# A hybrid decoder layer on one core: the opening loop's instruction order pinned on TensorE, ScalarE and VectorE, and the last shift sum moved to TensorE

## The chip, the cores and the metric

The kernel runs on 1 core of one Trainium2 chip. The metric is device time of one execution in microseconds; lower is better. The kernel before takes 2865.55 us, the median of 3 runs (2865.07 to 2865.57). The profile shown here is of one further execution, which took 2869.29 us.

## The reference, cut to what matters

One decoder layer over 512 tokens of 2048 channels, in float32. The opening stage, which the change touches, computes the normalised and conditioned input `h` and its first products:

```python
mod = jax.nn.silu(c) @ w_ada + b_ada
shift, scale, gate = jnp.split(mod[:, None, :], 3, axis=-1)
h = rms_norm(x, norm_w) * (1.0 + scale) + shift
proj = h @ w_in
```

Behind it stand a sliding-window attention branch, a gated delta-rule branch and their gated merge, all of which read `h`. `c` is one vector of 2048, so `silu(c) @ w_ada` is a product of one row with a 2048 x 6144 matrix: every weight is loaded for one multiplication.

## The kernel before, in words

`h` is kept transposed: channels on the 128 partitions, in `KT` = 16 channel tiles of 128, and the 512 tokens along the free side. A product in float32 is made of three matmuls. Each operand is split into a rounded high part and the remainder (`whi` and `wlo` of the weights, `hh` and `hl` of `h`), and the kernel adds `hh*whi`, `hl*whi` and `hh*wlo` in PSUM. ScalarE makes the high part by a copy, and VectorE the low part by a subtraction that reads it.

The function `startup` is the opening stage. It loads `x` in four blocks, normalises and transposes it into `xnT` (up to about 28 us), and then walks the 16 channel tiles. For tile `kt` these steps are needed:

- **The sums** (line 450, and 441 to 447). Two numbers for each of the tile's 128 channels: index `j` = 0 is the shift, 1 the scale. Each is a dot product of 2048 weights with `silu(c)`. On VectorE one is a multiplication over a 128 x 2048 tile `wa` with an accumulated output, written here as sum(kt, j). The shift of even tiles is instead made on TensorE: 16 small matmuls into the PSUM tile `ada` (line 441), a copy to `adas` by ScalarE (446), and a last matmul with the vector `pick` that adds four partial rows (447). For those tiles the weights are stored in another layout.
- **adaln(kt)** (lines 455 to 469). Two VectorE instructions on 128 x 1, here sh0 (line 459, the shift) and sh1 (line 463, the scale), then on ScalarE `h` (468) and its rounded copy `hh` (469).
- **low(kt)** (line 473): `hl` on VectorE.
- **The weight split**: `whi` (line 53, ScalarE) and `wlo` (line 54, VectorE) of the tile's 128 x 832 weights of `w_st`, one half of a load `raw`.
- **products(kt)**: seven outputs accumulate in PSUM over all 16 tiles: two value tiles `v`, one tile `ba`, four key tiles `k`. With three matmuls each that is 21 matmuls per tile (lines 275 to 277).

In the loop, pass `kt` writes adaln(kt+1), the sums of kt+2, low(kt+1) and the products of kt. That is only the order in which the source names them. A scheduler of the framework then sets the order on each engine by its own estimate of when things are ready, and the engines run their lists in that order, each waiting at its next instruction until its inputs are there.

The weights of the sums come in 32 loads of 1 MB into six buffers `wa`; the loads for tile kt+3 go into the buffers of tile kt, so their issue waits until sum or matmuls of tile kt have read them. The loads `raw` (832 KB, one for two tiles) have two buffers; the issue waits for the second `wlo` of the load two before. All are issued by SyncE's queue in order. After the loop come `ba`, the two `vt` copies and the next stage (`mm` tiles, lines 275 to 277 again), in which TensorE works through the large weight matrices.

Of the kernel before, what the change touches and what calls it, by code (L numbers as in the profile page):

```python
# [36 lines left out]

class Layer:
# [339 lines left out]
    def startup(self, st):  # L378


        tc, nc, a, const = self.tc, self.nc, self.a, self.const
# [4 lines left out]

        def load_ada(kt):
            for j in range(2):
                wa = s2.tile([P, D], F32, tag="wa", name="wa", bufs=6)
# [22 lines left out]
        scr = sp.tile([P, KT, 32], F32, name="silu_cr")  # L412
        nc.vector.tensor_copy(out=scr, in_=self.sc.unsqueeze(2).to_broadcast([P, KT, 32]))
        scb = sp.tile([P, D], F32, name="silu_cb")
        for q in range(4):
# [4 lines left out]
            nc.scalar.copy(out=scb[:, q * T : (q + 1) * T], in_=ps.rearrange("p c n -> p (c n)"))  # L420
        pick = sp.tile([P, 1], F32, name="pick")
        nc.vector.memset(pick, 0.0)
        for g in range(4):
# [7 lines left out]
        ada = pa.tile([P, T], F32, name="ada")

        def ada_sums(kt):


            t = acc[kt] = s2.tile([P, 2], F32, tag="acc", name="acc")
            if kt % 2 == 0:
                w = loads[kt, 0].rearrange("p (k n) -> p k n", k=KT)
                for k in range(4):
                    for g in range(4):  # L440
                        nc.tensor.matmul(
                            ada[32 * g : 32 * g + 32, 0:P], lhsT=scr[:, 4 * k + g, :], rhs=w[:, 4 * k + g, :],
                            start=k == 0, stop=k == 3,
                        )
                sb = s2.tile([P, P], F32, tag="adas", name="adas", bufs=1)
                nc.scalar.copy(out=sb, in_=ada[:, 0:P])
                nc.tensor.matmul(ada[:, P : P + 1], lhsT=sb, rhs=pick, start=True, stop=True)
            for j in (1, 0)[: 1 + kt % 2]:
                wa = loads[kt, j]
                nc.vector.scalar_tensor_tensor(  # L450
                    out=wa, in0=wa, scalar=1.0, in1=scb, op0=ALU.mult, op1=ALU.mult, accum_out=t[:, j : j + 1]
                )
                yield

        def adaln(kt):

            t = acc[kt]
            sh = s2.tile([P, 2], F32, tag="sh", name="sh")
            nc.vector.tensor_scalar(
                out=sh[:, 0:1], in0=t[:, 0:1] if kt % 2 else ada[:, P : P + 1], scalar1=self.b_ada[:, kt : kt + 1],  # L460
                scalar2=None, op0=ALU.add,
            )
            nc.vector.tensor_scalar(
                out=sh[:, 1:2], in0=t[:, 1:2], scalar1=self.norm_w[:, kt : kt + 1], scalar2=bn[:, kt : kt + 1],
                op0=ALU.mult, op1=ALU.add,
            )
            h32 = s2.tile([P, T], F32, tag="h32", name="h32")
            nc.scalar.activation(h32, xnT[:, kt, :], AF.Identity, scale=sh[:, 1:2], bias=sh[:, 0:1])
            nc.scalar.copy(out=self.hh[:, kt, :], in_=h32)
            return h32  # L470

        def low(kt, h32):
            nc.vector.tensor_tensor(
                out=self.hl[:, kt, :], in0=h32, in1=self.hh[:, kt, :].bitcast(F32), op=ALU.subtract
            )

        n = 0
        for tb in range(NTB):
# [8 lines left out]
            for q in range(4):  # L487
                i = n % 7
                ps = pa.tile([P, 4, P], F32, tag=f"x{i}", name="xtp") if i < 3 else self.psc.tile([P, 4, P], F32, tag="sc", name="xtp")
# [6 lines left out]
                    nc.scalar.copy(out=dst, in_=ps)  # L496
                n += 1

        def products(kt, parts):
            f, l = kt == 0, kt == KT - 1  # L500
            wh, wl = parts
            x = (self.hh[:, kt, :], self.hl[:, kt, :])
            for ps, o, n in outs:
                self.mm3(ps, (wh[:, o : o + n], wl[:, o : o + n]), x, f, l)

        list(ada_sums(0))
        low(0, adaln(0))
        list(ada_sums(1))
# [1280 lines left out]
```

## Time and profile before

| What | Value |
|---|---|
| Median of 3 runs | 2865.55 us |
| The profiled execution | 2869.29 us, span 2867.5 us |
| TensorE busy, share of the span | 2819.6 us, 98% |
| VectorE, ScalarE, GpSimd busy | 64%, 41%, 9% |
| Data moved | 590.09 MB, mean 206 GB/s |
| First matmul of the loop's products | 31.29 us |
| First matmul of the next stage (`mm`) | 144.55 us |
| VectorE multiplications of 128 x 2048 (line 450) | 24, mean 2283 ns |

Times in the trace count from the start of the span. A row of the timeline has the start, the duration, the engine, the line, the operation and the tiles (written before read, buffer numbers left out). A bracket behind it says how long the engine was idle before that row and what ended the wait. Durations overlap in the engines' pipelines, so the cost of an instruction in a row of them is the distance from its start to the next start, not its own duration.

### The profile page before, as it was taken

How to read it: one execution, taken by the hardware profiler on the slowest of the kernel's cores; microseconds unless marked ns; L12 is line 12 of the kernel's file. 1: busy time of each engine (PE TensorE's matmuls, PEld its weight loads, DVE VectorE, ACT ScalarE, POOL GpSimd, SP SyncE). 2: the span in 40 equal slices, each digit the busy share in tenths (PEclk: the TensorE clock that was granted, in tenths of full speed). 3: DMA queues.
4: the chain of work that ended last, by engine and by line, in shares of the span. 5: the costliest groups of instructions: out<-in, count | busy, mean ns of one | idle time of the engine just before them, and what ended most of it. 6: DMA issues, size and time to landing. Idle time of an engine off the chain costs nothing.

```text
span 2867.5 us, 38132 instructions
## 1 busy us (share of the span) xinstructions
PE 2819.6 (98%) x14364; PEld 2321.4 (81%) x14364; DVE 1824.3 (64%) x2882; ACT 1176.7 (41%) x2289; POOL 271.1 (9%) x266
## 2 busy tenths in 40 slices
PE   7899999999999999999999999999999999999999
PEld 6687788788888888888888888888887778788887
DVE  6765988877775555566665456666556655554575
ACT  4354333344444444444443455443343434442343
POOL 0022111101102111111100000000100100000000
PEclk9999999999999999999999999999999999999999
DMA  9757555636768777878873477675645647365575
GB/s 377 291 190 204 171 174 156 199 103 198 222 195 249 204 229 232 252 232 245 248 209 102 145 257 264 242 258 187 224 149 164 176 140 218 121 226 176 203 233 163
DMA packets 205807, 590.09 MB, mean 206 GB/s; under 512 B 74900, under 2 KB 99988, under 8 KB 154424
## 3 DMA queue, kind: packets, MB, share of 16 engines
q1 hardware_dynamic: 195416, 529.46, 54.1%
q0 software_dynamic: 10208, 58.20, 10.5%
q8 instruction: 113, 1.85, 0.3%
q14 instruction: 70, 0.57, 0.1%
HBM read 523.79 MB, written 166.40 MB: 241 GB/s over the span
## 4 chain that ended last, share of the span: by engine, by line
PE 88%; DVE 6%; DMA 2%; ACT 2%; issue 1%; SPq 0%; POOL 0%; DVEq 0%; POOLq 0%; ACTq 0%
PE mm L275 21%; PE mm L277 20%; PE mm L276 20%; PE od L276 3%; PE od L275 3%; PE od L277 3%; PE m L277 2%; PE m L276 2%; PE m L275 2%; DVE wa L450 1%; PE S L1425 1%; DVE wlo L54 1%; DVE A L886 1%; PE po L1057 1%; DVE atmp L879 1%; PE O L1476 1%
## 5 line engine op out<-in xcount | busy, mean ns | idle before, releaser
L275 PE MATMUL mm<-hh,whi 128*128 128x512 f32 x2784 | 1125.0, 404 | 5.5 <-ACT mth L298 4.6
L277 PE MATMUL mm<-hh,wlo 128*128 128x512 f32 x2784 | 1089.7, 391 | 2.7 <-DVE wlo L54 2.7
L276 PE MATMUL mm<-hl,whi 128*128 128x512 f32 x2784 | 1088.0, 391 | 0.0
L54 DVE TENSOR_TENSOR wlo<-raw,whi 128x1024 fp32r<-128x1024 f32 (+1 forms) x476 | 586.9, 1236 | 504.5 <-ACT whi L53 503.1
L53 ACT CAST whi<-raw 128x1024 fp32r<-128x1024 f32 (+1 forms) x476 | 496.8, 1047 | 797.1 <-PE mm L276 651.5
L275 PEld LDWEIGHTS mm<-hh,whi 128*128 128x128 f32 x2784 | 524.4, 188 | 118.9 <-issue 9.6
L277 PEld LDWEIGHTS mm<-hh,wlo 128*128 128x128 f32 x2784 | 523.4, 188 | 116.3 <-DVE wlo L54 3.9
L276 PEld LDWEIGHTS mm<-hl,whi 128*128 128x128 f32 x2784 | 524.9, 189 | 102.6 <-issue 1.4
L276 PE MATMUL od<-wlo,oh 128*128 128x512 f32 x448 | 174.6, 390 | 0.4 <-DVE wlo L54 0.4
L275 PE MATMUL od<-whi,oh 128*128 128x512 f32 x448 | 174.8, 391 | 0.0
L277 PE MATMUL od<-whi,ol 128*128 128x512 f32 x448 | 174.4, 389 | 0.0
L834 POOL TENSOR_TENSOR E<-E,neg_g 128x512 f32<-128x512 f32 x64 | 74.5, 1163 | 928.3 <-DMA E<-g_rows 804.6
L886 DVE TENSOR_TENSOR A<-A,atmp 128x62 f32<-128x62 f32 (+30 forms) x124 | 113.6, 916 | 1.7
L879 DVE TENSOR_TENSOR atmp<-A 128x62 f32<-128x62 f32 (+30 forms) x124 | 112.9, 911 | 1.6
L276 PEld LDWEIGHTS od<-wlo,oh 128*128 128x128 f32 x448 | 84.1, 188 | 17.9 <-DVE wlo L54 0.8
L277 PEld LDWEIGHTS od<-whi,ol 128*128 128x128 f32 x448 | 84.1, 188 | 17.6
L275 PEld LDWEIGHTS od<-whi,oh 128*128 128x128 f32 x448 | 84.1, 188 | 17.1
L54 DVE TENSOR_TENSOR wlo<-raww,whi 128x1024 fp32r<-128x1024 f32 x56 | 68.4, 1223 | 45.5 <-ACT whi L53 45.4
L53 ACT CAST whi<-raww 128x1024 fp32r<-128x1024 f32 x56 | 59.2, 1057 | 81.8 <-PE m L277 71.9
L988 POOL TENSOR_TENSOR qe<-qe,yq 128x512 f32<-128x512 f32 x32 | 49.8, 1577 | 420.1 <-DMA qe<-eg_rows 249.5
L1059 ACT COPY osb<-po 128x256 f32<-128x256 f32 x64 | 23.9, 373 | 126.9 <-PE po L1057 126.8
L1043 ACT ACTIVATE vs<-pv,kd 128x128 f32<-128x128 f32 x96 | 30.1, 366 | 107.0 <-PE pv L1039 107.0
(341 smaller groups left out, 3273.2 us busy)
## 6 DMA issues: line engine op xcount, KB each, us to landing
raw<-in_w_ch SPq DMA_DIRECT2D x158, 1024.0 KB
wa<-in_w_ada_ss SPq DMA_DIRECT2D x32, 1024.0 KB
od_m<-in_w_od POOLq DMA_DIRECT2D x32, 1024.0 KB, 10.9
raw<-od_m SPq DMA_DIRECT2D x32, 1024.0 KB
raw<-in_w_od SPq DMA_DIRECT2D x24, 1024.0 KB
E<-g_rows SPq DMA_DIRECT2D x64, 256.0 KB
od_m<-in_w_od SPq DMA_DIRECT2D x16, 1024.0 KB
od_m<-od_m SPq DMA_DIRECT2D x16, 1024.0 KB
```

Source lines behind the costliest of these rows:

```text
L53: self.nc.scalar.copy(out=hi, in_=src)
L54: self.nc.vector.tensor_tensor(out=lo, in0=src, in1=hi.bitcast(F32), op=ALU.subtract)
L275: nc.tensor.matmul(ps, lhsT=wh, rhs=xh, start=first, stop=False)
L276: nc.tensor.matmul(ps, lhsT=wh, rhs=xl, start=False, stop=False)
L277: self.last_mm = nc.tensor.matmul(ps, lhsT=wl, rhs=xh, start=False, stop=last).ins
L450: nc.vector.scalar_tensor_tensor(out=wa, in0=wa, scalar=1.0, in1=scb, op0=ALU.mult, op1=ALU.mult, accum_out=t[:, j : j + 1])
L834: self.in_turn(nc.gpsimd.tensor_tensor(out=E, in0=E, in1=ng, op=ALU.add))
L879: eng.tensor_tensor(out=t, in0=A[:, m : m + 1, m + 1 :].to_broadcast([P, m, n]), in1=A[:, :m, m : m + 1].to_broadcast([P, m, n]), op=ALU.mult,
L886: eng.tensor_tensor(out=A[:, :m, m + 1 :], in0=A[:, :m, m + 1 :], in1=t, op=ALU.add)
L988: self.in_turn(nc.gpsimd.tensor_tensor(out=qf, in0=qf, in1=q, op=ALU.mult))
L1043: nc.scalar.activation(vs[:, e, :], pv[:, e, :], AF.Copy, scale=self.kd[:, c, 2 * g + e : 2 * g + e + 1])
L1057: m = nc.tensor.matmul(po[:, e, :], lhsT=M[e][:, c, :], rhs=vn[:, e, :], start=c == 0, stop=True)
```

## The change

A helper `turn` adds an ordering edge from each instruction to the last one given to it for the same engine; the edge asks for an order only, not for a wait. With it the loop's order is written out for three engines:

- **VectorE**, in pass kt: sh1(kt+1), sh0(kt+1), wlo(kt+1), hl(kt+1), then the sums of kt+2.
- **ScalarE**: whi(kt+1), the copy `adas` where tile kt+1 has its shift on TensorE, h(kt+1), hh(kt+1).
- **TensorE**: the 16 small matmuls of tile kt+1, then the products of kt, output by output with the order `hh*whi`, `hl*whi`, `hh*wlo`; the matmul with `pick` stands after the first two outputs.

Only one half of weights is split ahead, where the scheduler was free to take several. Of the last tile, 15, the shift sum moves from VectorE to TensorE (`SHIFT_PE`), so VectorE has 23 multiplications of 128 x 2048 in place of 24. After the loop one split of weights is made as before. The core of the diff:

```diff
+SHIFT_PE = (0, 2, 4, 6, 8, 10, 12, 14, 15)
...
+        def turn(op, queue="dve"):
+
+            if queue in last:
+                self.tc.add_manual_dep(
+                    op.ins, last[queue],
+                    mybir.DependencyInfo(mybir.DependencyClass.NoSync, mybir.DependencyReason.DATA), reason="turn",
+                )
+            last[queue] = op.ins.name
+
+        def shift_sum(kt):
+
+
+            if kt not in SHIFT_PE:
+                return
...
+                    turn(nc.tensor.matmul(
+                        ada[32 * g : 32 * g + 32, 0:P], lhsT=scr[:, 4 * k + g, :], rhs=w[:, 4 * k + g, :],
+                        start=k == 0, stop=k == 3,
+                    ), "pe")
+            sb = s2.tile([P, P], F32, tag="adas", name="adas", bufs=1)
+            turn(nc.scalar.copy(out=sb, in_=ada[:, 0:P]), "act")
+            return sb
...
-            for j in (1, 0)[: 1 + kt % 2]:
+            for j in (1,) if kt in SHIFT_PE else (0, 1):
                 wa = loads[kt, j]
-                nc.vector.scalar_tensor_tensor(
+                turn(nc.vector.scalar_tensor_tensor(
                     out=wa, in0=wa, scalar=1.0, in1=scb, op0=ALU.mult, op1=ALU.mult, accum_out=t[:, j : j + 1]
-                )
-                yield
+                ))
...
+            weights(kt, parts)
+            turn(nc.vector.tensor_tensor(
                 out=self.hl[:, kt, :], in0=h32, in1=self.hh[:, kt, :].bitcast(F32), op=ALU.subtract
-            )
+            ))
...
+            for i, (ps, o, n) in enumerate(outs):
+                if i == 2:
+                    to_channels(sb)
+                for a, b in ((wh, x[0]), (wh, x[1]), (wl, x[0])):
+                    m = nc.tensor.matmul(
+                        ps, lhsT=a[:, o : o + n], rhs=b, start=f and b is x[0] and a is wh, stop=l and a is wl
+                    )
+                    turn(m, "pe")
...
         for kt in range(KT):
-            nxt = kt + 1 < KT and adaln(kt + 1)
+            parts = kt + 1 < KT and cast(kt + 1)
             if kt + 3 < KT:
                 load_ada(kt + 3)
-            sums = ada_sums(kt + 2) if kt + 2 < KT else iter(())
-            next(sums, None)
-            if kt + 1 < KT:
-                low(kt + 1, nxt)
-            list(sums)
-            products(kt, self.half(f"st{kt // 2}"))
-            self.half_done()
+            products(kt, shift_sum(kt + 1))
+            if parts:
+                adaln(kt + 1, parts)
+            if kt + 2 < KT:
+                sums(kt + 2)
             self.weight_tick()
+        self.split_half()
```

VectorE's list from hl(7) to hl(9), in the kernel before. `hl` with `h32` is a tile's low part, `wa` with `acc` a sum, `sh` from `ada` or from `acc` with `b_adaT` is sh0, `sh` with `norm_wT` is sh1:

```order
L473 TENSOR_TENSOR hl_68<-h32_679,hh_67 128x512
L459 TENSOR_SCALAR sh_733<-ada_175,b_adaT_105 128x1
L450 SCALAR_TENSOR_TENSOR wa_643,acc_686<-wa_643,silu_cb_140 128x2048
L463 TENSOR_SCALAR sh_733<-acc_686,norm_wT_107,bn_171 128x1
L54 TENSOR_TENSOR wlo_771<-raw_670,whi_770 128x832
L54 TENSOR_TENSOR wlo_828<-raw_670,whi_827 128x832
L473 TENSOR_TENSOR hl_68<-h32_736,hh_67 128x512
L450 SCALAR_TENSOR_TENSOR wa_682,acc_743<-wa_682,silu_cb_140 128x2048
L459 TENSOR_SCALAR sh_774<-acc_743,b_adaT_105 128x1
L450 SCALAR_TENSOR_TENSOR wa_684,acc_743<-wa_684,silu_cb_140 128x2048
L463 TENSOR_SCALAR sh_774<-acc_743,norm_wT_107,bn_171 128x1
L473 TENSOR_TENSOR hl_68<-h32_777,hh_67 128x512
```

The same stretch, hl(7) to hl(9), in the changed kernel:

```order
L507 TENSOR_TENSOR hl_68<-h32_707,hh_67 128x512
L470 SCALAR_TENSOR_TENSOR wa_623,acc_712<-wa_623,silu_cb_140 128x2048
L495 TENSOR_SCALAR sh_763<-acc_712,norm_wT_107,bn_171 128x1
L499 TENSOR_SCALAR sh_763<-ada_175,b_adaT_105 128x1
L484 TENSOR_TENSOR wlo_717<-raw_616,whi_716 128x832
L507 TENSOR_TENSOR hl_68<-h32_766,hh_67 128x512
L470 SCALAR_TENSOR_TENSOR wa_679,acc_771<-wa_679,silu_cb_140 128x2048
L470 SCALAR_TENSOR_TENSOR wa_681,acc_771<-wa_681,silu_cb_140 128x2048
L495 TENSOR_SCALAR sh_802<-acc_771,norm_wT_107,bn_171 128x1
L499 TENSOR_SCALAR sh_802<-acc_771,b_adaT_105 128x1
L484 TENSOR_TENSOR wlo_775<-raw_616,whi_774 128x832
L507 TENSOR_TENSOR hl_68<-h32_805,hh_67 128x512
```

The work is the same: three sums, two `wlo`, two `hl`. Before, both `wlo` stand in the step to the even tile and none in the step to the odd one. Now each step has one, between sh0 and `hl`.

TensorE's list at the start of products(7) in the kernel before, from the small matmuls of tile 8 on:

```order
L441 MATMUL ada_175<-wa_641,silu_cr_138 32x128 x16
L275 MATMUL v0_371<-hh_67,whi_729 128x512
L275 MATMUL v1_372<-hh_67,whi_729 128x512
L447 MATMUL ada_175<-pick_165,adas_703 128x1
L276 MATMUL v0_371<-hl_68,whi_729 128x512
L277 MATMUL v0_371<-hh_67,wlo_730 128x512
```

The same place in the changed kernel:

```order
L453 MATMUL ada_175<-wa_719,silu_cr_138 32x128 x16
L541 MATMUL v0_375<-hh_67,whi_774 128x512
L541 MATMUL v0_375<-hl_68,whi_774 128x512
L541 MATMUL v0_375<-hh_67,wlo_775 128x512
L541 MATMUL v1_376<-hh_67,whi_774 128x512
L541 MATMUL v1_376<-hl_68,whi_774 128x512
L541 MATMUL v1_376<-hh_67,wlo_775 128x512
L463 MATMUL ada_175<-pick_165,adas_837 128x1
```

The second matmul of the products now reads `hl`, where it was the third or a later one, and the matmul with `pick` stands behind six matmuls in place of two. SyncE's list of loads keeps its order except that the third `raw` load now stands ahead of the two loads for tile 4. Behind the loop the lists differ in a few places of the gate computation and in the place of one `raw` load only.

More of the change, by code (lines that the diff above doesn't have):

```diff
@@ L431, in startup @@
         ada = pa.tile([P, T], F32, name="ada")
-        def ada_sums(kt):
-            t = acc[kt] = s2.tile([P, 2], F32, tag="acc", name="acc")
[L437 to L443, printed above, removed]
-                        )
-                sb = s2.tile([P, P], F32, tag="adas", name="adas", bufs=1)
-                nc.scalar.copy(out=sb, in_=ada[:, 0:P])
-                nc.tensor.matmul(ada[:, P : P + 1], lhsT=sb, rhs=pick, start=True, stop=True)
-            for j in (1, 0)[: 1 + kt % 2]:
+        last = {}
@@ new lines, in turn @@
+        def turn(op, queue="dve"):
[8 more added lines that the diff above has]
+                return
+            w = loads[kt, 0].rearrange("p (k n) -> p k n", k=KT)
+            for k in range(4):
+                for g in range(4):
+                    turn(nc.tensor.matmul(
[5 more added lines that the diff above has]
+            return sb
@@ L449, in ada_sums, with to_channels, sums @@
+        def to_channels(sb):
+            if sb is not None:
+                turn(nc.tensor.matmul(ada[:, P : P + 1], lhsT=sb, rhs=pick, start=True, stop=True), "pe")
+        def sums(kt):
+            t = acc[kt] = s2.tile([P, 2], F32, tag="acc", name="acc")
+            for j in (1,) if kt in SHIFT_PE else (0, 1):
                 wa = loads[kt, j]
-                nc.vector.scalar_tensor_tensor(
+                turn(nc.vector.scalar_tensor_tensor(
                     out=wa, in0=wa, scalar=1.0, in1=scb, op0=ALU.mult, op1=ALU.mult, accum_out=t[:, j : j + 1]
-                )
@@ L453, in ada_sums, with cast, weights @@
-                yield
-        def adaln(kt):
+                ))
+        def cast(n):
+            w = self.jobs[n // 2][1].shape[-1] // 2
+            hi = self.whl.tile([P, 1024], F32R, tag="whi", name="whi")
+            lo = self.whl.tile([P, 1024], F32R, tag="wlo", name="wlo")
+            src = self.raws[n // 2][:, (n % 2) * w : (n % 2 + 1) * w]
+            turn(nc.scalar.copy(out=hi[:, :w], in_=src), "act")
+            return hi, lo, src, w
+        def weights(n, parts):
+            hi, lo, src, w = parts
+            turn(nc.vector.tensor_tensor(out=lo[:, :w], in0=src, in1=hi[:, :w].bitcast(F32), op=ALU.subtract))
+            self.halves[n] = (hi, lo)
+            self.half_split += 1
+            if n % 2:
+                del self.raws[n // 2], self.raw_in[n // 2]
+                self.due.append(self.load_job)
@@ L457, in adaln @@
+        def adaln(kt, parts):
             t = acc[kt]
             sh = s2.tile([P, 2], F32, tag="sh", name="sh")
[L459 to L463, printed above, removed]
+            turn(nc.vector.tensor_scalar(
                 out=sh[:, 1:2], in0=t[:, 1:2], scalar1=self.norm_w[:, kt : kt + 1], scalar2=bn[:, kt : kt + 1],
@@ L465, in adaln @@
                 op0=ALU.mult, op1=ALU.add,
-            )
-            h32 = s2.tile([P, T], F32, tag="h32", name="h32")
[L468 to L473, printed above, removed]
+            ))
+            turn(nc.vector.tensor_scalar(
+                out=sh[:, 0:1], in0=ada[:, P : P + 1] if kt in SHIFT_PE else t[:, 0:1],
+                scalar1=self.b_ada[:, kt : kt + 1], scalar2=None, op0=ALU.add,
+            ))
@@ L474, in low @@
+            h32 = s2.tile([P, T], F32, tag="h32", name="h32")
+            turn(nc.scalar.activation(h32, xnT[:, kt, :], AF.Identity, scale=sh[:, 1:2], bias=sh[:, 0:1]), "act")
+            turn(nc.scalar.copy(out=self.hh[:, kt, :], in_=h32), "act")
+            weights(kt, parts)
+            turn(nc.vector.tensor_tensor(
                 out=self.hl[:, kt, :], in0=h32, in1=self.hh[:, kt, :].bitcast(F32), op=ALU.subtract
-            )
+            ))
         n = 0
@@ L497, in startup, with products @@
                 n += 1
-        def products(kt, parts):
+        def products(kt, sb):
             f, l = kt == 0, kt == KT - 1
-            wh, wl = parts
+            wh, wl = self.halves.pop(kt)
             x = (self.hh[:, kt, :], self.hl[:, kt, :])
[L503 to L508, printed above, removed]
+            for i, (ps, o, n) in enumerate(outs):
[6 more added lines that the diff above has]
+                    turn(m, "pe")
+                self.last_mm = m.ins
+            self.half_used += 1
+        to_channels(shift_sum(0))
+        parts = cast(0)
+        sums(0)
+        adaln(0, parts)
+        sums(1)
         acc_v = [pa.tile([P, T], F32, tag=f"x{i}", name=f"v{i}") for i in range(2)]
@@ L1720, in layout @@
     ss = w_ada[:, : 2 * D].T.reshape(2, KT, P, D).transpose(1, 0, 2, 3).copy()
-    ss[0::2, 0] = ss[0::2, 0].reshape(-1, P, KT, P).transpose(0, 3, 2, 1).reshape(-1, P, D)
+    on_pe = list(SHIFT_PE)
+    ss[on_pe, 0] = ss[on_pe, 0].reshape(-1, P, KT, P).transpose(0, 3, 2, 1).reshape(-1, P, D)
     o["w_ada_ss"] = ss
```

## Prediction

> **What bounds the kernel now.** I read the busy time of the engines by stage first. Columns are the stretch, then its length, then busy time with instruction counts of PE, PEld, DVE, ACT and POOL, the granted TensorE clock, the DMA share and GB/s:
>
> ```profile
> 31.20:144.50 113.30, 96.96 (x574) 71.22 (x575) 84.94 (x111) 35.46 (x55) 0.00 (x0) 0.93 0.82 323
> 144.50:500.00 355.50, 347.40 (x1621) 286.43 (x1621) 282.09 (x448) 144.07 (x295) 68.25 (x68) 1.00 0.58 178
> 1400.00:2867.50 1467.50, 1458.62 (x7280) 1193.86 (x7278) 850.36 (x1327) 596.23 (x1022) 82.85 (x87) 1.00 0.60 193
> ```
>
> After 144.5 us TensorE is the bound: 347.4 busy of 355.5, then 1458.6 of 1467.5. In the loop it is busy 97 of 113.3 us, at a granted clock of 0.93. So a microsecond taken from the loop should come off the whole, if the stages behind keep their own pace. The waits of that stretch (waiter, releaser, total, times, longest) say who holds it up:
>
> ```profile
> ACT h L468 <- DVE sh L463: 63.6, 15, 6.2
> PE v L275 <- ACT hh L469: 18.7, 14, 3.3
> ```
>
> The chain is VectorE's sums, then `sh`, then ScalarE's `h` and `hh`, then TensorE. VectorE's timeline for one pair of tiles, hl(7) to hl(9):
>
> ```profile
> 82.11 0.69 DVE L473 TENSOR_TENSOR hl<-h,hh 128x512 fp32r<-128x512 f32 x1 [1.53 <-ACT hh L469]
> ...
> 83.15 2.28 DVE L450 SCALAR_TENSOR_TENSOR wa<-wa,silu_cb 128x2048 f32<-128x2048 f32 x1
> ...
> 85.48 0.27 DVE L463 TENSOR_SCALAR sh<-acc,norm_wT,bn 128x1 f32<-128x1 f32 x1
> 85.67 1.02 DVE L54 TENSOR_TENSOR wlo<-raw,whi 128x832 fp32r<-128x832 f32 x1
> 87.42 1.03 DVE L54 TENSOR_TENSOR wlo<-raw,whi 128x832 fp32r<-128x832 f32 x1 [0.74 <-ACT whi L53]
> 88.36 0.69 DVE L473 TENSOR_TENSOR hl<-h,hh 128x512 fp32r<-128x512 f32 x1
> 88.96 2.29 DVE L450 SCALAR_TENSOR_TENSOR wa<-wa,silu_cb 128x2048 f32<-128x2048 f32 x1
> ...
> 91.42 2.28 DVE L450 SCALAR_TENSOR_TENSOR wa<-wa,silu_cb 128x2048 f32<-128x2048 f32 x1
> ...
> 95.56 0.69 DVE L473 TENSOR_TENSOR hl<-h,hh 128x512 fp32r<-128x512 f32 x1 [1.53 <-ACT hh L469]
> ```
>
> A pair takes 95.56 - 82.11 = 13.45 us: 6.25 to the even tile, 7.20 to the odd one. VectorE idles 1.53 us ahead of hl(9) for ScalarE, with nothing to do; ahead of hl(8) it does both `wlo`, and waits 0.74 between them because the second `whi` comes late. ScalarE beside it:
>
> ```profile
> 85.78 0.82 ACT L468 ACTIVATE h<-xnT,sh 128x512 f32<-128x512 f32 x1 [2.75 <-DVE sh L463]
> 86.51 0.88 ACT L53 CAST whi<-raw 128x832 fp32r<-128x832 f32 x1
> ...
> 94.06 0.82 ACT L468 ACTIVATE h<-xnT,sh 128x512 f32<-128x512 f32 x1 [6.16 <-DVE sh L463]
> 94.91 0.62 ACT L469 CAST hh<-h 128x512 fp32r<-128x512 f32 x1
> ```
>
> **The change, term by term.** Distances of starts, from these rows: hl to the next sum 0.60 (88.36 to 88.96); a sum to what follows 2.33 (83.15 to 85.48); sh1 to the next VectorE instruction 0.19 (85.48 to 85.67); sh to h 0.30 (85.48 to 85.78); h to hh 0.85 (94.06 to 94.91); hh to hl 0.65 (94.91 to 95.56). In the pinned order a step from hl to hl is therefore 0.60 + 2.33 s + 0.19 + 0.30 + 0.85 + 0.65 = 2.59 + 2.33 s, with s sums: 4.92 us to an even tile (s = 1), 7.25 to an odd one (s = 2), 12.17 a pair in place of 13.45. The `wlo` (0.94 to its successor, 87.42 to 88.36) costs nothing here: from sh0 to hl VectorE waits 1.80 us anyway, and its `whi` was made in the pass before, since ScalarE's list puts it right behind the last hh. If that cover goes, it is 0.94 a step.
>
> Term B, hl(1) to hl(14): these are tiles 1 to 14, 13 steps. Before (the rows below) it is 128.69 - 42.56 = 86.13 us. After, 7 short and 6 long steps: 34.44 + 43.50 = 77.94, and 0.4 for the first step, in which two small conversions of constants stand in the list and the matmul with `pick` is late behind products(0): 78.3. Gain 7.8.
>
> Term A, up to hl(1). VectorE, then ScalarE:
>
> ```profile
> 31.69 0.69 DVE L473 TENSOR_TENSOR hl<-h,hh 128x512 fp32r<-128x512 f32 x1
> ...
> 39.82 1.03 DVE L54 TENSOR_TENSOR wlo<-raw,whi 128x832 fp32r<-128x832 f32 x1 [2.78 <-ACT whi L53]
> ...
> 42.56 0.69 DVE L473 TENSOR_TENSOR hl<-h,hh 128x512 fp32r<-128x512 f32 x1 [1.53 <-ACT hh L469]
> ...
> 128.69 0.68 DVE L473 TENSOR_TENSOR hl<-h,hh 128x512 fp32r<-128x512 f32 x1
> ...
> 137.31 0.68 DVE L473 TENSOR_TENSOR hl<-h,hh 128x512 fp32r<-128x512 f32 x1
> ```
>
> ```profile
> 28.30 0.89 ACT L53 CAST whi<-raw 128x832 fp32r<-128x832 f32 x1
> 29.13 0.82 ACT L468 ACTIVATE h<-xnT,sh 128x512 f32<-128x512 f32 x1
> ...
> 38.90 0.89 ACT L53 CAST whi<-raw 128x832 fp32r<-128x832 f32 x1 [7.66 <-PE k L276]
> ```
>
> At 38.90 ScalarE had been stuck 7.66 us in a fourth `whi` whose buffer products(0) still held; VectorE's `wlo` behind it stood ahead of sh1(1), so all of tile 1 waited. The pinned order splits one half ahead, and this stall goes. h(0) stays at 29.13 (whi(0) takes the place at 28.30); hh(0) follows at 29.98, hl(0) at 30.63, two sums from 31.23 to 35.89, then 0.19 + 0.30 + 0.85 + 0.65: hl(1) at 37.88, against 42.56. Gain 4.7.
>
> Term C, hl(14) to hl(15): before 137.31 - 128.69 = 8.62. One sum fewer on VectorE takes 2.33; what replaces it is 16 small matmuls on TensorE (a row below). They stand ahead of products(14), and TensorE is still in products(13) when hl(14) is ready, so `pick` and sh0(15) come later: by the paces below, TensorE ends products(13) 0.8 us after hl(14) starts, then 1.1 for the small ones, 1.4 for six matmuls, 0.3 for `pick`, 3.6 in all, where VectorE could go on at 0.60 + 2.33 + 0.19 = 3.1. So 0.5 is lost: gain 1.8. Bounds 0 (all lost) and 2.3.
>
> Term D, hl(15) to the next stage. TensorE there, and at the start of products(7):
>
> ```profile
> 136.71 1.22 PE L275 MATMUL v<-hh,whi 128*128 128x512 f32 x2 [3.33 <-ACT hh L469]
> ...
> 142.06 0.63 PE L275 MATMUL k<-hh,whi 128*128 128x512 f32 x1
> 142.48 0.63 PE L276 MATMUL k<-hl,whi 128*128 128x512 f32 x1
> ...
> 144.55 0.39 PE L275 MATMUL mm<-hh,whi 128*128 128x512 f32 x1
> ```
>
> ```profile
> 78.99 0.39 PE L276 MATMUL k<-hl,whi 128*128 128x512 f32 x1
> 79.22 0.39 PE L277 MATMUL k<-hh,wlo 128*128 128x512 f32 x1
> 79.54 1.08 PE L441 MATMUL ada<-wa,silu_cr 128*32 128x128 f32 x32
> 82.13 0.73 PE L275 MATMUL v<-hh,whi 128*128 128x512 f32 x2 [1.51 <-ACT hh L469]
> ```
>
> A matmul takes 0.23 us in the loop (78.99 to 79.22), but 0.42 after the idle 3.33 us (142.06 to 142.48): TensorE fell to half pace, and products(15) with it. From hl(15) to the first `mm` is 7.24 us. After the change TensorE is idle about 0.6 us there, so products(15) should run at full pace: 0.85 from hl to the first matmul that reads it (estimated from hl's 0.68 and a hand-over), then 20 x 0.23 = 4.6, together 5.45. Gain 1.8; 0 if the half pace stays.
>
> Sum: 4.7 + 7.8 + 1.8 + 1.8 = 16.1 us. The profiled execution would go from 2869.29 (span 2867.5) to 2853.2; it lies 3.74 above the median, which I carry over: 2865.55 - 16.1 = 2849.4, so I say **2849.5 us**, 0.56% faster. A measurement here can tell about 0.2%, 5.7 us.
>
> Do the other resources allow 12.17 us a pair? TensorE: 42 x 0.23 = 9.7, small matmuls 1.1, `pick` 0.3: 11.1. DMA, by stretch:
>
> ```profile
> 67.50:78.00 10.50, 8.83 (x38) 6.63 (x39) 8.31 (x12) 4.18 (x7) 0.00 (x0) 1.00 1.01 421
> 78.00:79.70 1.70, 1.70 (x16) 1.14 (x18) 1.70 (x2) 0.00 (x0) 0.00 (x0) 1.00 0.55 92
> ```
>
> A pair needs four loads of 1 MB and one `raw`: 4 x 1.049 + 0.852 = 5.05 MB. At 421 GB/s that is 12.0 us. In the present 13.45 it runs dry for 1.7 once. At 12.17 it fits, just; this is the nearest next bound. The new order on TensorE (the second matmul reads hl) makes it wait about 0.7 us more at each start. That is free while a step has slack: 12.17 - 11.1 = 1.1 us a pair.
>
> **The rivals.** *DMA sets the pace.* SyncE issues each `raw` only when the pair's second `wlo` is done, with four `wa` loads behind it. Were each pair still to run dry for 1.7 us, with the loop waiting for the data, it would take 12.0 + 1.7 = 13.7, and term B falls by 6 x 1.5 = 9: 2858.5. For it: 12.0 against 12.17. Against: the dry time is what the slower loop leaves over. From a raw's release at about hl(k), k odd, that load and the two for tile k+3 need 1.7 + 2.95 MB / 0.421 = 8.7 us; their sum starts at 12.17 + 0.60 = 12.8. About 4 us of cover would have to go first. Chance 0.10.
>
> *Given back later.* The next stage is paced by its own lists, but VectorE is busy 282 of 355 us there; if its solves started no earlier, TensorE would wait for them, and up to 16 us return: 2865.5. Against: TensorE idles 8.1 us in that stretch, and all its work hangs on the end of the loop. Chance 0.05.
>
> *Slower: TensorE at half pace throughout.* A pinned order leaves it idle once in each pair: 7.25 - 4.83 - 1.1 = 1.3 us. If such a gap were enough to halve the pace, as 3.33 us did, products would take 21 x 0.42 = 8.8 us a tile: from TensorE's end of products(0) at about 38.6, 15 x 8.8 + 8 x 1.4 = 143 to 182, against 144.55, so 37 us slower: 2902. It decides from two half-pace spells of about 14 matmuls a pair on (2 x 14 x 0.19 = 5.3 on TensorE's 11.1, 4.2 above 12.17, 30 us over seven pairs, more than the gain). Against: 1.51 us ahead of 82.13 left the pace alone; and here is where it did not:
>
> ```profile
> 31.29 1.22 PE L275 MATMUL v<-hh,whi 128*128 128x512 f32 x2 [2.46 <-ACT hh L469]
> ...
> 34.02 0.63 PE L277 MATMUL v<-hh,wlo 128*128 128x512 f32 x1
> 34.44 0.63 PE L276 MATMUL v<-hl,whi 128*128 128x512 f32 x1
> ```
>
> So the point lies between 1.51 and 2.46 us. Chance 0.04. [...]
>
> **How the numbers follow.** The forecast has 0.81, the rivals 0.10, 0.05 and 0.04. Its own bounds: C and D lost make 3.6 us (2853); `pick` late by up to 0.5 in each of six even steps adds 3 (2856); downward, sh to h at 0.25 in place of 0.30 and fewer waits behind the loop, of 8 us there, some 5 (2844.5). With the DMA case the range is 2844.5 to 2859.5. Chances: faster by over 0.2% is the forecast and nearly all of the DMA case, 0.90; within 0.2% 0.06; slower 0.04.
>
> **What would show it.** Right: hl(1) near 37.9, steps of 4.9 and 7.25 between `hl` rows, hl(14) near 116, the first `mm` near 128.5, no `wlo` that waits, no idle of VectorE on a `wa` load, a clock near 1.00 from 40 us on. Wrong: sums that wait for DMA (first rival), equal steps but a late end of the key stage (second), matmuls 0.42 apart in the middle of the loop (third), sh0 waiting for `pick` by more than 0.5 us.

## The result, and the profile after

The changed kernel takes 2849.38 us (median of 6 runs, 2846.98 to 2851.82); the kernel before, on the same chip, 2865.56 us (6 runs, 2863.34 to 2868.93). The ratio is 0.9942, 95% interval 0.9932 to 0.9951: 16.2 us less, with an interval of 14 to 19.5 us. The profiled execution of the changed kernel took 2849.35 us, with a span of 2847.1 us.

Its busy time by stage, in the columns of the prediction's first view (length, busy time of PE, PEld, DVE, ACT, POOL, granted TensorE clock, DMA share, GB/s):

```profile
31.20:128.00 96.80, 93.40 (x614) 69.93 (x615) 82.61 (x110) 38.23 (x57) 0.00 (x0) 0.98 0.93 375
128.00:483.50 355.50, 348.08 (x1624) 286.83 (x1625) 282.66 (x449) 144.03 (x297) 71.02 (x68) 1.00 0.59 181
```

TensorE is now busy in 93.4 of 96.8 us of the loop, where it was 97 of 113.3. DMA went from a share of 0.82 to 0.93. The 355.5 us behind the loop have the same work and 7.4 us of idle TensorE against 8.1: nothing came back there. From the first `mm` to the end of the span the old kernel took 2722.95 us, the new one 2720.65.

What was waited for between 28 and 145 us (total, times, longest):

```profile
ACT h L504 <- DVE sh L499: 52.2, 15, 4.8
DVE hl L507 <- ACT hh L505: 8.8, 15, 0.6
PE v L541 <- ACT hh L505: 3.6, 6, 1.8
```

The chain is still VectorE's sums, `sh`, `h`, `hh`, `hl`, but TensorE's waiting for `hh` fell from 18.7 to 3.6 us (1.8 us for `hl` are new), and VectorE waits at most 0.6 us for `hh`. VectorE's pair of tiles from hl(7) to hl(9):

```profile
73.45 0.69 DVE L507 TENSOR_TENSOR hl<-h,hh 128x512 fp32r<-128x512 f32 x1 [0.60 <-ACT hh L505]
74.06 2.28 DVE L470 SCALAR_TENSOR_TENSOR wa<-wa,silu_cb 128x2048 f32<-128x2048 f32 x1
...
76.57 0.21 DVE L499 TENSOR_SCALAR sh<-ada,b_adaT 128x1 f32<-128x1 f32 x1
...
78.32 0.69 DVE L507 TENSOR_TENSOR hl<-h,hh 128x512 fp32r<-128x512 f32 x1 [0.61 <-ACT hh L505]
78.93 2.28 DVE L470 SCALAR_TENSOR_TENSOR wa<-wa,silu_cb 128x2048 f32<-128x2048 f32 x1
...
81.14 2.28 DVE L470 SCALAR_TENSOR_TENSOR wa<-wa,silu_cb 128x2048 f32<-128x2048 f32 x1
...
83.47 0.27 DVE L495 TENSOR_SCALAR sh<-acc,norm_wT,bn 128x1 f32<-128x1 f32 x1
83.66 0.20 DVE L499 TENSOR_SCALAR sh<-acc,b_adaT 128x1 f32<-128x1 f32 x1
...
85.40 0.69 DVE L507 TENSOR_TENSOR hl<-h,hh 128x512 fp32r<-128x512 f32 x1 [0.60 <-ACT hh L505]
```

The steps are 4.87 and 7.08 us, a pair 11.95 in place of 13.45. `sh` (76.57) no longer waits for `pick`. VectorE at both ends of the loop:

```profile
30.36 0.69 DVE L507 TENSOR_TENSOR hl<-h,hh 128x512 fp32r<-128x512 f32 x1 [0.38 <-ACT hh L505]
...
37.45 0.69 DVE L507 TENSOR_TENSOR hl<-h,hh 128x512 fp32r<-128x512 f32 x1 [0.60 <-ACT hh L505]
...
114.18 0.69 DVE L507 TENSOR_TENSOR hl<-h,hh 128x512 fp32r<-128x512 f32 x1 [0.60 <-ACT hh L505]
...
117.83 0.22 DVE L499 TENSOR_SCALAR sh<-ada,b_adaT 128x1 f32<-128x1 f32 x1 [0.43 <-PE ada L463]
...
119.87 1.22 DVE L55 TENSOR_TENSOR wlo<-raw,whi 128x1024 fp32r<-128x1024 f32 x1 [0.90 <-ACT whi L54]
121.02 0.68 DVE L507 TENSOR_TENSOR hl<-h,hh 128x512 fp32r<-128x512 f32 x1
```

These are hl(0), hl(1), hl(14), sh0(15), a `wlo` of the next stage, and hl(15). That `wlo` stood there in the kernel before too (136.17). It waits 0.90 us for its `whi`, which ScalarE makes at 118.81 us between h(15), at 118.08, and hh(15), at 119.74. TensorE at the end of the loop:

```profile
121.76 0.50 PE L541 MATMUL v<-hl,whi 128*128 128x512 f32 x1 [0.26 <-DVE hl L507]
...
126.23 0.39 PE L541 MATMUL k<-hh,wlo 128*128 128x512 f32 x1
126.45 0.39 PE L276 MATMUL mm<-hh,whi 128*128 128x512 f32 x1
```

The last products run 0.22 to 0.23 us apart, where they were 0.42 apart, and the first `mm` comes at 126.45 in place of 144.55. DMA by stretch:

```profile
50.00:54.00 4.00, 3.78 (x18) 3.00 (x18) 3.77 (x6) 1.52 (x4) 0.00 (x0) 1.00 0.85 284
...
102.00:114.00 12.00, 11.42 (x78) 8.58 (x77) 10.68 (x14) 4.66 (x8) 0.00 (x0) 1.00 1.01 421
114.00:118.00 4.00, 4.00 (x47) 3.00 (x46) 3.35 (x6) 1.21 (x3) 0.00 (x0) 1.00 0.22 90
```

From 54 to 114 us DMA is full: a share of 1.01 at 419 GB/s. It no longer runs dry once in each pair, and no VectorE instruction of the loop waits for it.

### The profile page after: what moved, and what is told of

It reads as the page before. It is cut to its first block, busy times and chain, and to the rows that moved or that the text cites. A ratio compares the mean times of both kernels' runs of the same rounds, so it can differ in the third digit from the quotient of the medians.

```text
span 2847.1 us, 38183 instructions
## 1 busy us (share of the span) xinstructions
PE 2815.1 (99%) x14398; PEld 2318.9 (81%) x14398; DVE 1818.7 (64%) x2880; ACT 1175.3 (41%) x2290; POOL 277.4 (10%) x266
## 3 DMA queue, kind: packets, MB, share of 16 engines
q8 instruction: 113, 1.85, 0.3%
## 4 chain that ended last, share of the span: by engine, by line
PE 87%; DVE 6%; DMA 2%; ACT 2%; issue 1%; POOL 0%; SPq 0%; DVEq 0%; POOLq 0%; ACTq 0%
PE mm L276 20%; PE mm L278 20%; PE mm L277 20%; PE od L277 3%; PE od L276 3%; PE od L278 3%; PE m L276 2%; PE m L278 2%; PE m L277 2%; DVE wa L470 2%; PE S L1468 1%; PE po L1100 1%; PE O L1519 1%; PE pv L1082 1%; DVE wlo L55 1%
## 5 line engine op out<-in xcount | busy, mean ns | idle before, releaser
L55 DVE TENSOR_TENSOR wlo<-raw,whi 128x1024 fp32r<-128x1024 f32 x460 | 569.6, 1241 | 492.8 <-ACT whi L54 492.0
L54 ACT CAST whi<-raw 128x1024 fp32r<-128x1024 f32 x460 | 481.9, 1050 | 785.1 <-PE mm L277 644.2
L1102 ACT COPY osb<-po 128x256 f32<-128x256 f32 x64 | 23.8, 372 | 126.9 <-PE po L1100 126.9
```

Of the source, the lines that this page charges most:

```text
L54: self.nc.scalar.copy(out=hi, in_=src)
L55: self.nc.vector.tensor_tensor(out=lo, in0=src, in1=hi.bitcast(F32), op=ALU.subtract)
```

## The experiments

All of them change the kernel before or the changed kernel by a few lines. The table has the start of some instructions in the profiled execution, the distance from hl(0) to the first `mm` (profiled executions start the loop up to 1.9 us apart), and the time against the kernel before, measured beside each run on the same chip (so a ratio isn't the median divided by 2865.56).

| Run | hl(1) | hl(14) | hl(15) | first mm | mm - hl(0) | Median, us | Ratio and interval |
|---|---|---|---|---|---|---|---|
| before | 42.56 | 128.69 | 137.31 | 144.55 | 112.86 | 2865.56 | |
| after | 37.45 | 114.18 | 121.02 | 126.45 | 96.09 | 2849.38 | 0.9942 (0.9932 to 0.9951) |
| only_dve | 38.92 | 121.02 | 127.65 | 133.49 | 103.35 | 2855.28 | 0.9956 (0.9939 to 0.9972) |
| only_act | 40.23 | 131.37 | 139.16 | 143.52 | 111.62 | 2865.19 | 0.9992 (0.9983 to 1.0002) |
| only_pe | 43.04 | 140.43 | 148.44 | 155.45 | 124.11 | 2876.04 | 1.0033 (1.0023 to 1.0043) |
| shift_only | 42.22 | 128.30 | 136.16 | 140.49 | 109.23 | 2861.88 | 0.9983 (0.9974 to 0.9992) |
| warm_tail | 41.01 | 127.08 | 135.70 | 140.02 | 108.76 | 2865.77 | 1.0001 (0.9991 to 1.0010) |
| pin_tail | 37.22 | 114.06 | 119.41 | 125.74 | 95.60 | 2849.26 | 0.9941 (0.9929 to 0.9954) |
| pin_tail_no15 | 37.44 | 114.17 | 121.25 | 126.70 | 96.34 | 2853.76 | 0.9961 (0.9947 to 0.9974) |
| more_dma | 37.40 | 125.32 | 131.51 | 136.93 | 106.61 | 2862.17 | 0.9988 (0.9979 to 0.9997) |
| sum_between | 37.48 | 113.83 | 121.11 | 126.54 | 96.14 | 2848.82 | 0.9940 (0.9925 to 0.9956) |
| combo | 37.55 | 114.94 | 119.81 | 125.39 | 94.92 | 2848.70 | 0.9940 (0.9927 to 0.9953) |
| combo2 | 39.14 | 113.31 | 119.23 | 125.56 | 93.50 | 2847.63 | 0.9935 (0.9921 to 0.9949) |

### Which engine's order matters

Three runs write the order down for one engine only and leave the others to the scheduler; all keep the shift of tile 15 on TensorE and the changed kernel's source order. No run pins two of the three.

```diff
-            if queue in last:
+            if queue == "dve" and queue in last:
```

> The changed kernel with the ordering edges on VectorE alone; ScalarE and TensorE are left to the scheduler. Theory (order on VectorE shortens the steps, order on ScalarE removes the early stall): ScalarE again splits up to four halves ahead, so h(1) waits for the fourth as before (hl(1) near 40 instead of 37.5), and in each step to an odd tile a weight copy stands between h and hh (0.65 us more, 7.7 for 7.1). First mm matmul at 133 +- 1.5, time about 2856. Rival (VectorE's list is the whole gain): first mm at 126.5, time about 2849. Rival (only all three together gain): first mm above 140.

VectorE alone gave a pair of 12.60 us and the first `mm` at 133.49, as expected, and some two thirds of the gain (a part of which is tile 15's, see shift_only). VectorE's rows hl(8) and hl(9):

```profile
83.23 0.69 DVE L507 TENSOR_TENSOR hl<-h,hh 128x512 fp32r<-128x512 f32 x1 [0.61 <-ACT hh L505]
...
90.95 0.69 DVE L507 TENSOR_TENSOR hl<-h,hh 128x512 fp32r<-128x512 f32 x1 [1.24 <-ACT hh L505]
```

The even step is 4.88 as in the changed kernel; the odd one is 7.72 against 7.08, and its `hl` waits 0.64 us longer for `hh`. On ScalarE a `whi` (89.53) stands between `h` (88.81) and `hh` (90.30), as expected.

```diff
-            if queue in last:
+            if queue == "act" and queue in last:
```

> The changed kernel with the ordering edges on ScalarE alone. Theory: the stall of tile 1 goes (hl(1) near 38), since one half is split ahead; VectorE, left to the scheduler, puts a wlo behind each hl and a sum into the wait for h and hh, which makes about 12.35 us a pair for 11.95. First mm matmul at 130 +- 1.5, time about 2853. Rival (VectorE's list is the whole gain): first mm above 138.

This missed: no gain that can be measured, with the first `mm` at 143.52. The stall of tile 1 did shrink: hl(1) comes 8.33 us behind hl(0), against 10.87 before. VectorE from the `wlo` behind hl(7) to hl(8), in the order that the scheduler made for it in this run:

```profile
81.87 1.02 DVE L484 TENSOR_TENSOR wlo<-raw,whi 128x832 fp32r<-128x832 f32 x1
84.60 0.22 DVE L499 TENSOR_SCALAR sh<-ada,b_adaT 128x1 f32<-128x1 f32 x1 [1.70 <-PE ada L463]
...
87.06 0.27 DVE L495 TENSOR_SCALAR sh<-acc,norm_wT,bn 128x1 f32<-128x1 f32 x1
...
89.46 0.69 DVE L507 TENSOR_TENSOR hl<-h,hh 128x512 fp32r<-128x512 f32 x1
```

The scheduler now sets sh0 of the even tile ahead of both sums. There it waits 1.70 us for `pick` with the sums queued behind it, and a sum stands between sh1 (87.06) and `hl` (89.46). A pair takes 14.17 us. I had expected a `wlo` behind each `hl` and a sum in the wait for `h` and `hh`, and both came; the place of sh0, and with it the wait for `pick`, I had not foreseen.

```diff
-            if queue in last:
+            if queue == "pe" and queue in last:
```

> The changed kernel with the ordering edges on TensorE alone. Theory: it brings none of the gain but the sum moved in the last step, and costs, since VectorE's list keeps sh0 of an even tile right behind hl of the odd one, and the matmul with pick now comes 1.6 us later: steps no shorter than before, hl(1) near 42, first mm matmul at 143 +- 2, time about 2864. Rival (any fixed order helps by itself): first mm below 138.

That this order alone brings no gain was right, but I had put the first `mm` at 143 and the time at 2864, slightly better than before. The first `mm` is at 155.45, 10.9 us later than before, and the time is 0.33% longer. VectorE, and the stretch of two tiles (with the granted clock behind the five busy times):

```profile
86.42 1.03 DVE L484 TENSOR_TENSOR wlo<-raw,whi 128x832 fp32r<-128x832 f32 x1 [2.06 <-ACT whi L479]
...
89.68 0.22 DVE L499 TENSOR_SCALAR sh<-ada,b_adaT 128x1 f32<-128x1 f32 x1 [1.63 <-PE ada L463]
```

```profile
85.00:100.00 15.00, 12.46 (x74) 8.59 (x73) 10.67 (x14) 4.61 (x7) 0.00 (x0) 0.89 0.92 354
```

`wlo` waits 2.06 us for a `whi` whose buffer TensorE still reads (between 28 and 156 us ScalarE waits 23.8 us in 8 such waits), sh0 waits 1.63 us for a `pick` that is pinned late, and the clock falls in parts of the loop (0.89 in this stretch). So by itself the order on TensorE is a cost. The three runs give 0.44%, 0.08% and -0.33%, the three orders together 0.58%: the gain isn't a sum of three parts. Whether the orders on VectorE and ScalarE alone would give all of it, without TensorE's, was not run and stays open.

### The last tile and the hand-over to the next stage

**shift_only** moves the shift sum of tile 15 in the kernel before, without any ordering edge; the layout of that tile's weights in DRAM changes with it.

```diff
+SHIFT_PE = (0, 2, 4, 6, 8, 10, 12, 14, 15)
...
-            for j in (1, 0)[: 1 + kt % 2]:
+            for j in (1,) if kt in SHIFT_PE else (1, 0):
...
-                out=sh[:, 0:1], in0=t[:, 0:1] if kt % 2 else ada[:, P : P + 1],
+                out=sh[:, 0:1], in0=ada[:, P : P + 1] if kt in SHIFT_PE else t[:, 0:1],
```

> The kernel before with nothing changed but the shift sum of tile 15 on TensorE. Theory: the last step loses one sum of 2.4 us, and the idle time ahead of products(15) falls from 3.33 to about 1 us, so its matmuls run at full pace and another 1.8 come off: first mm matmul at 140.3 instead of 144.55, time about 2861.3. Rival (pace unchanged): only 2.4 us, first mm at 142.2. Rival (pick late, as the sum of the prediction has it): at least 0.5 of the 2.4 is lost.

VectorE, hl(14), sh0(15) and hl(15):

```profile
128.30 0.68 DVE L474 TENSOR_TENSOR hl<-h,hh 128x512 fp32r<-128x512 f32 x1
130.46 0.22 DVE L460 TENSOR_SCALAR sh<-ada,b_adaT 128x1 f32<-128x1 f32 x1 [1.48 <-PE ada L448]
...
136.16 0.68 DVE L474 TENSOR_TENSOR hl<-h,hh 128x512 fp32r<-128x512 f32 x1
```

The last step is 7.86 us against 8.62: it lost 0.76 us, not 2.4, because sh0(15) stands ahead of the sum and waits 1.48 us for `pick`, so the last rival was right. The first `mm` follows 4.33 us later against 7.24, since the last products run 0.23 us apart behind an idle gap of 1.14 us. The gap was as expected, but the gain from it is 2.9 us, not 1.8. The two misses cancel, so that the first `mm` at 140.49 is near the forecast 140.3 by luck. The time fell by 0.17%: this small part of the change takes 4.1 us off the first `mm` by itself, 0.4 of it from an earlier hl(0).

**warm_tail** takes only the idle gap away: ten matmuls into `ada` that nobody reads, between the products of tiles 14 and 15 of the kernel before.

```diff
+            if kt == KT - 1:
+                with self.behind():
+                    for _ in range(10):
+                        nc.tensor.matmul(ada, lhsT=self.hh[:, 12, 0:P], rhs=self.hh[:, 12, :], start=True, stop=True)
```

> The kernel before with ten matmuls of 128x512 added between products(14) and products(15), which nothing reads: about 2.3 us of work in the 3.33 us in which TensorE was idle. Theory (the idle time alone puts products(15) at half pace): hl(15) unchanged at 137.3, products(15) 0.23 us apart, first mm matmul at 142.7 instead of 144.55. [...]

TensorE in products(15):

```profile
136.58 0.40 PE L276 MATMUL v<-hl,whi 128*128 128x512 f32 x1
136.82 0.40 PE L277 MATMUL v<-hh,wlo 128*128 128x512 f32 x1
```

The pace is 0.23 to 0.24 us in place of 0.42, and hl(15) to the first `mm` is 4.32 in place of 7.24, a gain of 2.9 us where I had expected 1.85. So the half pace there came from the idle time. The gain isn't seen in the time, though: the first `mm` came 4.5 us sooner than before, part of it from an earlier start, and the median is the same. In this profile the part behind the first `mm` took 2724.6 us, the longest of all (2719 to 2724 in the others), and the ten runs lie between 2862.3 and 2870.4. Why it doesn't show stays open.

**pin_tail** adds to the changed kernel that the first split of the next stage stands behind hl(15). **pin_tail_no15** also puts the shift of tile 15 back on VectorE.

```diff
-        self.split_half()
+        weights(KT, cast(KT))
```

> The changed kernel with one more split pinned: the first half of the next stage's weights, which the scheduler put between h(15) and hh(15) on ScalarE and ahead of hl(15) on VectorE, now follows hl(15). Theory: hl(15) comes 1.75 us behind sh0(15) instead of 3.06, so products(15) and the first mm matmul come 1.3 us earlier, 125.1 for 126.45, and the new wlo is ready in time under products(15): time about 2848. Rival (the next stage then waits for its wlo): first mm at 126.5 or later.

> pin_tail with the shift sum of tile 15 back on VectorE. Theory (the sum moved is worth one VectorE sum less the lateness of pick, 0.4): hl(14) to hl(15) 7.1 us for 5.5, idle time ahead of products(15) stays under 2 us and the pace full, first mm matmul at 126.7, 1.7 later than pin_tail. Rival (pace falls to half ahead of products(15)): 3.5 later. Rival (TensorE ends last anyway): no change.

In pin_tail hl(15) comes 1.5 us sooner behind hl(14) than in the changed kernel (5.35 against 6.84), but the first `mm` follows 6.33 us behind it rather than 5.43: TensorE is then still in products(14). From hl(0) on 0.5 us is left, and nothing in the time. Without the shift of tile 15 on TensorE the first `mm` comes 0.7 us later from hl(0) on. It came at the 126.7 that I had expected, but the distance to pin_tail was to be larger: pin_tail gained less than I thought. The medians lie 4.5 us apart, more than the landmarks; the intervals of the two ratios overlap.

### How near DMA is

**more_dma** adds to the changed kernel a copy of 512 KB per pass in DRAM, in the queue of the loads; its result isn't used.

```diff
+        extra = self.dram.tile([KT, P, 1024], F32, name="extra")
...
+                nc.sync.dma_start(out=extra[kt], in_=a["w_ada_ss"][kt, 0][:, 0:1024])
```

> The changed kernel with one further copy of 512 KB per pass for passes 0 to 12, from the weights to a scratch tensor in DRAM that nothing reads, on the same queue. Estimated from 421 GB/s it takes 1.25 us each, 16 us in all. Theory (DMA is already busy 12.0 of 11.95 us a pair and only some 2 to 4 us of cover stand between it and the loop): VectorE's sums wait for wa loads, pairs of about 14.4 us, first mm matmul at 138 +- 4, time about 2861. Rival (DMA has slack, VectorE sets the pace alone): first mm within 1 us of 126.5.

VectorE, hl(9), the sum behind it, and hl(11):

```profile
89.15 0.69 DVE L508 TENSOR_TENSOR hl<-h,hh 128x512 fp32r<-128x512 f32 x1 [0.60 <-ACT hh L506]
92.22 2.29 DVE L471 SCALAR_TENSOR_TENSOR wa<-wa,silu_cb 128x2048 f32<-128x2048 f32 x1 [2.38 <-DMA wa<-in_w_ada_ss]
...
103.56 0.69 DVE L508 TENSOR_TENSOR hl<-h,hh 128x512 fp32r<-128x512 f32 x1 [0.60 <-ACT hh L506]
```

A pair takes 14.41 us, the sums wait 2.38 us a pair for their data, and of the gain of 0.58% a rest of 0.12% is left. DMA then sets the pace, as expected.

**sum_between** uses the time in which VectorE waits for `h` and `hh` of the even tile: the first sum of the next odd tile stands between `wlo` and `hl`.

```diff
-                adaln(kt + 1, parts)
+                split = kt % 2 and kt + 2 < KT - 1
+                adaln(kt + 1, parts, (lambda: sums(kt + 2, (0,))) if split else None)
```

> The changed kernel with one move on VectorE: in each step to an even tile the first of the next odd tile's two sums stands between wlo and hl, in place of the wait of 0.6 us. Theory: VectorE alone would need 11.35 us a pair, but TensorE starts the even products later, its small matmuls and pick fall behind, and sh0 of the even tile waits for pick: about 11.9 us a pair, first mm matmul within 1 us of 126.45. Rival (VectorE sets the pace alone): 11.35 a pair, first mm at 123.

The first `mm` came at 126.54, as expected, but for a reason that I had not named. The first pairs take 11.62 us; from 73 us on the sums wait, and the pairs are 11.95 to 11.97 again. VectorE:

```profile
85.58 2.29 DVE L474 SCALAR_TENSOR_TENSOR wa<-wa,silu_cb 128x2048 f32<-128x2048 f32 x1 [0.59 <-DMA wa<-in_w_ada_ss]
```

**combo** puts sum_between and pin_tail together, and makes the small matmuls one pass earlier, so that `pick` can stand behind the first output.

```diff
-                if i == 2:
+                if i == 1:
                     to_channels(sb)
+                if i == 5:
+                    shift_sum(kt + 2)
```

> The move of sum_between and of pin_tail together, with the small matmuls of an even tile one pass earlier (behind output 5 of the products two tiles before) and the matmul with pick behind the first output. Theory (DMA is the next bound): VectorE could go at 11.35 us a pair, but the loads need 12.0, so sums wait for wa loads late in the loop; the first mm matmul follows the landing of the last wa load by about 9.7 us: 122 +- 1.5, time about 2845. Rival (VectorE sets the pace alone, no waits for DMA): first mm at 121. Rival (no slack left on TensorE): first mm at 125 or later.

This lies 1.9 us beyond the range. The first `mm` at 125.39 fits the number of the last rival, but the delay is on VectorE: pairs of 11.26 us up to hl(8) at 77.87, then 11.69 and 11.98, where the sums wait 0.62 us a pair for DMA, and one wait more on VectorE, at sh0(14):

```profile
113.18 0.22 DVE L507 TENSOR_SCALAR sh<-ada,b_adaT 128x1 f32<-128x1 f32 x1 [2.86 <-PE ada L453]
```

The small matmuls of tile 15 write the PSUM tile `ada` in the pass in which sh0(14) reads another column of it, and sh0(14) was held until they ended. **combo2** leaves these 16, and the `pick` behind them, where the changed kernel has them:

```diff
-                if i == 1:
+                if i == (2 if l or kt + 2 == KT else 1):
                     to_channels(sb)
-                if i == 5:
+                if i == 5 and kt + 2 < KT - 1:
                     shift_sum(kt + 2)
...
+            if kt + 2 == KT:
+                shift_sum(KT - 1)
+                sb = shift_copy(KT - 1)
             products(kt, sb)
```

> As the run named combo, but the 16 small matmuls of tile 15 stand ahead of the products of tile 14, as in the changed kernel, and no longer ahead of the step that reads the pick result of tile 14. Theory A (that one PSUM wait of 2.86 us is what held combo back; DMA sets the pace of about 12.0 us a pair from 80 us on): hl(13) stays near 106.4, hl(14) comes at 111.4 to 112 in place of 114.9, hl(15) near 118, the first mm at 123.5 within 1, and the time about 2846.5 (2.5 us under the changed kernel, hardly more than its scatter). Theory B (the DMA transfers are late at that point anyway, so the wait only covered them): the sums of tile 14 or 15 wait for their loads instead, hl(15) stays at 119.5 or later, the first mm at 125 to 126.

VectorE from hl(13) to hl(14):

```profile
107.71 0.69 DVE L517 TENSOR_TENSOR hl<-h,hh 128x512 fp32r<-128x512 f32 x1 [0.60 <-ACT hh L513]
109.03 2.29 DVE L478 SCALAR_TENSOR_TENSOR wa<-wa,silu_cb 128x2048 f32<-128x2048 f32 x1 [0.63 <-DMA wa<-in_w_ada_ss]
...
113.31 0.69 DVE L517 TENSOR_TENSOR hl<-h,hh 128x512 fp32r<-128x512 f32 x1 [0.60 <-ACT hh L513]
```

This execution began its loop 1.59 us later than that of combo, so the distances count: hl(13) to hl(14) is 5.60 us in place of 8.54, and hl(0) to the first `mm` 93.50 in place of 94.92. The wait on `ada` was what held combo back there; theory A stands, with DMA's 0.63 us left in the step. Only 1.42 of the 2.94 us reach the first `mm`, among other things because sh0(15) now waits 0.87 us for `pick`. Of all kernels this has the lowest median, 2847.63 us, but its interval overlaps that of the changed kernel: the 2.6 us of the landmarks are about what these runs scatter.

## Why the prediction was right, and where it was off

The forecast was 2849.5 us, the median 2849.38. That is nearer than its terms deserve: they gave 16.1 us, the profile shows 18.1 up to the first `mm`, and the medians differ by 16.2 with an interval of 14 to 19.5. The two profiled executions differ by 19.9 us (2869.29 and 2849.35): that of before lay 3.7 above its median, that of after at its own. So the hit on the median is partly luck. The terms, one by one:

| Term | Forecast gain, us | Measured |
|---|---|---|
| A, up to hl(1) | 4.7 | 42.56 - 37.45 = 5.1 |
| B, hl(1) to hl(14) | 7.8 | 86.13 - 76.73 = 9.4 |
| C, hl(14) to hl(15) | 1.8 | 8.62 - 6.84 = 1.8 |
| D, hl(15) to the first `mm` | 1.8 | 7.24 - 5.43 = 1.8 |

- **A** was right in its mechanism: one half is split ahead, VectorE's `wlo` no longer holds the second tile, and the stall of 7.66 us is gone. The rest of 0.4 is hl(0), 0.27 sooner than I had it, and a step of 7.09 rather than 7.25. Of the 5.1 us, 3.8 lie between hl(0) and hl(1) (10.87 to 7.09); 1.3 are an earlier hl(0), whose place scatters between executions, so that part is less sure.
- **B** is the term that was mis-sized, by 1.6 us. The even steps were 4.87 against 4.92, the odd ones 7.08 against 7.25. I took 2.33 us for each sum, which is its distance to an instruction that reads its result. From one sum to the next it is 2.21 (78.93 to 81.14). And sh0 to `h` is 0.24 (83.66, then `h` at 83.90), not 0.30. Six odd steps make 1.0, the first step (5.01, not 5.3) 0.3, and the six other even ones 0.3.
- **C** was right with its parts: sh0(15) waited 0.43 us for `pick`, where I had put 0.5. shift_only and pin_tail_no15 show that it depends on what surrounds it: 0.8 us in the old order, where that wait is 1.48, and 0.7 by the first `mm` where the hand-over is pinned too.
- **D** was right, and warm_tail shows the cause: without the idle gap the half pace goes. It also splits the term: the half pace cost 2.9 us (7.24 to 4.32), and the new order, whose second matmul already needs `hl`, gives 1.1 of it back (5.43). That this gain is one in the whole time is not shown by itself, since warm_tail's median is that of before.
- **DMA** was rightly not the limit of this kernel, and rightly named as the next one. At an estimated 12.0 us a pair (5.05 MB at 421 GB/s) it has no room: more_dma loses most of the gain, and both versions with shorter steps fall back to 11.95 to 11.98 us.
- **Given back later** didn't happen: 2722.95 us behind the first `mm` before, 2720.65 after.
- **Half pace throughout** didn't happen in this kernel, but only_pe shows that spells of it can come within the loop: its clock of 0.89 between 85 and 100 us holds one of 3.4 us, not half pace throughout. My reason against it, a point between 1.51 and 2.46 us of idle time, was wrong; the last section shows executions that it does not fit.

## What to carry to other kernels

When you write the order of one engine down, look at the lists of the others again: here one engine's order gave two thirds of the gain, nothing, or a loss, and in only_act the scheduler had put an instruction that waits ahead of both sums on an engine left free. All three together gave the whole; two of them were not tried. Cost a step by the distances of starts in its own neighbourhood (a sum ahead of another sum took 2.21 us, ahead of its reader 2.33). And look at the pace of the data: with pairs of 11.95 us, where the loads need an estimated 12.0, shorter steps showed up here as waits for loads (0.59 us ahead of a sum in sum_between, 0.62 us a pair in combo).

## What the runs showed of the hardware

TensorE's half pace did not follow from the length of one idle gap. TensorE at the start of the loop in the changed kernel, and then in pin_tail_no15, which has the same order there:

```profile
30.38 0.51 PE L541 MATMUL v<-hh,whi 128*128 128x512 f32 x1 [1.81 <-ACT hh L505]
...
31.69 0.63 PE L541 MATMUL v<-hh,whi 128*128 128x512 f32 x1
32.11 0.63 PE L541 MATMUL v<-hl,whi 128*128 128x512 f32 x1
...
35.10 0.39 PE L541 MATMUL k<-hh,wlo 128*128 128x512 f32 x1
```

```profile
30.38 0.50 PE L541 MATMUL v<-hh,whi 128*128 128x512 f32 x1 [1.81 <-ACT hh L505]
...
31.67 0.39 PE L541 MATMUL v<-hh,whi 128*128 128x512 f32 x1
31.90 0.39 PE L541 MATMUL v<-hl,whi 128*128 128x512 f32 x1
```

The same gap of 1.81 us was followed by half pace (0.42 apart, up to 35.10) in one execution and by full pace in the other. And in only_pe two gaps of 0.8 us with one matmul between them were followed by half pace:

```profile
93.96 0.50 PE L541 MATMUL v<-hh,whi 128*128 128x512 f32 x1 [0.83 <-ACT hh L505]
95.28 0.50 PE L541 MATMUL v<-hl,whi 128*128 128x512 f32 x1 [0.81 <-DVE hl L507]
...
96.28 0.63 PE L541 MATMUL v<-hl,whi 128*128 128x512 f32 x1
...
99.26 0.39 PE L541 MATMUL k<-hh,wlo 128*128 128x512 f32 x1
```

The granted clock, read in slices of 0.2 us from 20 to 156 us, falls to half 23 times in twelve of these thirteen kernels, and each spell lasts 3.41 us or twice that: in the kernel before at 30.34, 44.00 and 136.16 us, for 6.83, 3.41 and 6.83 us. In only_pe the six falls, at 30.97, 44.62, 65.10, 95.82, 126.54 and 150.43 us, lie 4, 6, 9, 9 and 7 times 3.41 us apart, within 0.1 us. A fall does not come at a fixed time behind a gap: in the changed kernel the clock fell at 31.68, 1.3 us after the gap of 1.81 us had ended, and in pin_tail, behind a gap of the same length, at 30.07, just before its end.

Nor did the idle time just ahead decide it alone. Of the 3.41 us ahead of the four falls in the kernels before and after, TensorE was idle for 1.89, 1.99, 2.79 and 2.03 us; in pin_tail_no15 the stretch that answers to the last of these has the same two gaps, 1.81 and 0.22 us, and no fall behind it. What decides, and how much idle time it takes, these runs do not show; the single limit of the prediction does not fit them.
